# A decoder layer on one Trainium2 core: gated rows and weights of the last six down tiles go into the operand slots of the recursive units

## The chip, the cores and the metric

The kernel runs on one NeuronCore of a Trainium2 chip. The metric is the device time of one execution in microseconds (us), and the median of the runs counts. A time inside an execution is counted from the first instruction of the profiled execution.

## What is computed

One decoder layer runs over 1024 prompt tokens and 8 sample tokens (T = 1032 columns, width 1024). The change is in the last part of it, the gated feed-forward and the second layer norm:

```python
gt, up = jnp.split(h @ w_gate_up, 2, axis=-1)
h = layer_norm(ALPHA * h + (jax.nn.silu(gt) * up) @ w_down, ln2_g, ln2_b)
```

The feed-forward width is 2816, which is 22 tiles of 128 rows. All of it is float32 accuracy.

## The kernel before

**Number format.** TensorE multiplies float32r operands. Each operand x is kept as a pair: `hi`, a rounded copy that ScalarE casts (L79), and `lo = x - hi`, which VectorE subtracts (L80). `split` issues both. A product takes three matmuls: hi by hi, lo by hi and hi by lo (L120 to L122 in `mm3`, L245 to L247 in `fast_product`).

**The recursive units.** Most large products are made by a scheme of seven products on 2 x 2 blocks in place of eight. `gate_up_down` runs 28 such units one after the other: 20 for pairs of gate and up tiles (called `("g", f)`), then four for each of two parts of the down projection, (0, 0) to (0, 3) and (1, 0) to (1, 3). A part covers eight of the 22 gated tiles, and a unit of it makes two of the eight output row tiles. A unit has seven steps i = 0 to 6, each of 2 column halves p by 4 tiles by 3 matmuls of 258 columns. Steps 0, 2, 4 and 6 add into one PSUM bank per half (`ubf`), steps 1 and 5 into a second (`udf`), step 3 has a third (`ucf`). In between the banks are read: `p1s`, `p5s` and `u2s` are ScalarE copies (L271) after steps 0, 1 and 2, L273 on VectorE reads `ucf`, L275 reads `ubf` after step 4, L278 reads `udf` after step 5. So step 4 may not add to `ubf` before `u2s` is taken, and step 6 not before L275 has read it. At its end a unit adds its two row tiles to the running sum `scr_h` in DRAM with two accumulating DMAs on the GpSimd queue (L1425).

**The slots.** The moving operands of the down units lie in eight slots, called homes 0 to 7, each with one pair per column half. Product i of part q lies in home (i - q - 1) mod 8. So in part 1 the homes of steps 0 to 6 are 6, 7, 0, 1, 2, 3 and 4, and home 5, which step 6 of part 0 used, is empty during part 1. Homes 0, 3, 5 and 7 are the tiles of `quarter_pair`, the others are tiles `t1`, `t2`, `t4` and `t6` of the pool `tx`. `down_operand` fills the slots of part 1 during the units (0, 2) and (0, 3), with 14 loads of 516 KB (names `f1...` and `fs`) and 14 splits of 1032 columns.

**The last six tiles.** `LAST = (16, 6)`: gated tiles 16 to 21 are not in the two parts. `down` opens two new pools, `gA` for the six rows (128 x 1032, `gh` and `gl`) and `wl` for the weights, in the space that the slots leave when `tx` and the pools under it are closed. It loads the six rows (L1283), splits them by column chunk (384, 390 and 258 columns, `CH`), and `last_products` then makes for each chunk c and each output row tile m a sum `dl` of 18 matmuls (6 tiles by 3). In chunk 0 it also loads and splits the weights `wl` of tile m (two raw halves of 512 and 256 columns through six raw buffers, L95) and loads the running sum, `acc[m] <- scr_h` (L1309). VectorE adds `dl` to `acc` (L1326), and the layer norm of a chunk runs beside the next chunk. The last chunk has its own norm, `last_layer_norm`, after which the kernel ends.

**What sets the order.** In this part no order is written by hand. A list scheduler orders each engine's instructions by its own estimates, and each engine, and the SP queue that issues the loads, then works strictly in that order: an instruction that waits holds everything behind it on its engine. A new tile waits until the readers of the buffer that it takes over are done. `behind` pins one instruction behind another.

Of the kernel before, what the change touches and what calls it, by code (L numbers as in the profile page):

```python
# [10 lines left out]
F32 = mybir.dt.float32  # L11
# [7 lines left out]
P = 128  # L19
D = 1024  # L20
KT = D // P
# [40 lines left out]
class Builder:  # L62
# [910 lines left out]
    def last_layer_norm(self, n, r, product, gcol, emit):  # L973


        nc, ph = self.nc, self.ph
        ones = self.ones.bitcast(F32)
        tile_ = lambda tag, name, bufs, dt=F32: ph.tile([P, WIDE], dt, tag=tag, name=name, bufs=bufs)[:, :n]
        s1, s2 = tile_("s1", "ls1", 1), tile_("s2", "ls2", 1)
        hi, lo = (ph.tile([P, n], F32R, tag=f"c0{e}", name=f"c0{e}", bufs=1) for e in "hl")  # L980
        e1, e2 = self.bank("t", "le1")[:, :n], self.bank("t", "le2")[:, :n]

        def account(m):
            sq = s2 if m == 0 else tile_("sq", f"lsq{m}", 2)
            nc.scalar.activation(sq, r[m], AF.Square)
            if m == 7:
                return sq
            if m == 1:
                nc.vector.tensor_add(s1, r[0], r[1])
            elif m:  # L990
                nc.vector.tensor_add(s1, s1, r[m])
            if m:
                nc.gpsimd.tensor_add(s2, s2, sq)

        for m in range(KT):
            ps = product(m, last=m < LATE)
            if m in NORM_AT:
                self.norm_step()
            if m >= LATE:
                nc.tensor.matmul(ps, self.shift, hi, start=False, stop=False)  # L1000
                nc.tensor.matmul(ps, self.shift, lo, start=False, stop=True)
            nc.vector.scalar_tensor_tensor(r[m], ps, SHARE, r[m], op0=ALU.mult, op1=ALU.add)
            if m == 1:
                s = tile_("xres", "lc0", 2)
                nc.vector.tensor_add(s, r[0], r[1])
                self.split(hi, lo, s)
            elif m == LATE - 1:
                with self.tc.issue_after(self.last_mm):
                    c0 = self.bank("o", "c0")[:, :n]
                    nc.tensor.matmul(c0, self.shift, hi, start=True, stop=False)  # L1010
                    nc.tensor.matmul(c0, self.shift, lo, start=False, stop=True)
                for k in range(LATE):
                    nc.vector.scalar_tensor_tensor(r[k], c0, SHARE, r[k], op0=ALU.mult, op1=ALU.add)
                    account(k)
            elif m >= LATE:
                sq = account(m)
# [12 lines left out]
        self.norm_step()  # L1029
        for m in range(KT):  # L1030
            nc.vector.tensor_mul(r[m], r[m], rs)
            emit(m, r[m], self.vec[:, gcol + m:gcol + m + 1])
# [190 lines left out]
    def gate_up_down(self, ts):  # L1223
# [23 lines left out]
        for n, (u, i) in enumerate(todo):  # L1247
            if i == 1 and n // 7 + 1 < len(units):
                load(n // 7 + 1)
                with self.tc.issue_after(self.last_load):  # L1250
                    for _ in range(2):
                        next(copies, None)
            if n + ahead < len(todo):
                v, j = todo[n + ahead]
                self.fast_quarter(st[v], j)
            self.fast_step(st[u], i, moving[u[0]], finish[u])
            if i == 6:
                del st[u]
            if i in (1, 4) and sums and next(sums[0], self) is self:
                sums.popleft()  # L1260
            if u[0] == "g" and i == 6 and u[1] in (8, 16):
                sums.append(self.down_sums(u[1] // 8 - 1))
            nxt = 0 if u[0] == "g" else u[0] + 1
            if nxt < FAST:
                if u[1] == last[u[0]][1] - 1 and i == 3:
                    self.down_operand(nxt, 0, moving[nxt])
                if u == last[u[0]] and i < 6:
                    while sums:
                        for _ in sums.popleft():
                            pass  # L1270
                    self.down_operand(nxt, i + 1, moving[nxt])
        for _ in copies:
            pass

    def down(self, ga, wl):

        nc, io = self.nc, self.io
        f0, nf = LAST
        tiles = {j: [ga.tile([P, GS], F32R, tag=f"g{e}{j}", name=f"g{e}{f0 + j}", bufs=1) for e in "hl"]
                 for j in range(nf)}  # L1280
        g = [[tuple(a[:, t0:t0 + n] for a in tiles[j]) for t0, n in CH] for j in range(nf)]
        for j in range(nf):
            nc.sync.dma_start(tiles[j][1][:, :T].bitcast(F32), self.scr["f"][:, f0 + j, :])  # L1283
        last = None
        for c in range(3):
            for j in range(nf):
                hi, lo = g[j][c]
                ins = self.split(hi, lo, lo.bitcast(F32)), self.last_lo
                for a, b in zip(ins, last) if last else ():
                    self.behind(a, b)  # L1290
                last = ins
        acc = [self.zt(f"acc{m}") for m in range(KT)]
        self.last_products(acc, g, wl)

    def last_products(self, acc, g, pool):
        nc, io, ph = self.nc, self.io, self.ph
        self.norm, w = None, []
        f0, nf = LAST
        for c, (t0, n) in enumerate(CH):
            rs = [acc[m][:, t0:t0 + n] for m in range(KT)]  # L1300

            def product(m, last=True, c=c, n=n):
                if c == 0:
                    hi, lo = (pool.tile([P, nf * P], F32R, tag="wl", name=f"wl{e}{m}", bufs=16) for e in "hl")
                    for a, b in ((0, 512), (512, nf * P)):
                        raw = self.half_raw(io["wdn"][m][:, f0 * P + a:f0 * P + b], b - a, f"wl{m}r{a}")
                        self.split(hi[:, a:b], lo[:, a:b], raw[:, :b - a])
                    w.append([(hi[:, k * P:(k + 1) * P], lo[:, k * P:(k + 1) * P]) for k in range(nf)])
                    nc.sync.dma_start(acc[m], self.scr["h"][:, m, :])  # L1309
                ps = self.bank(("mm", "s")[m % 2], f"dl{m}_{c}")[:, :n]  # L1310
                self.mm3(ps, [(w[m][k], g[k][c]) for k in range(nf)], last)
                return ps

            def emit(m, v, scale=1.0, t0=t0, n=n):
# [4 lines left out]
                self.last_layer_norm(n, rs, product, V_G2, emit)  # L1319
                break  # L1320
            s1 = ph.tile([P, WIDE], F32, tag="s1", name=f"o2s{c}", bufs=1)[:, :n]
            for m, r in enumerate(rs):
                ps = product(m)
                if m in NORM_AT:
                    self.norm_step()
                nc.vector.scalar_tensor_tensor(r, ps, SHARE, r, op0=ALU.mult, op1=ALU.add)  # L1326
                if m == 1:
                    nc.vector.tensor_add(s1, rs[0], r)
                elif m > 1:
                    nc.vector.tensor_add(s1, s1, r)  # L1330
            self.norm_start(self.layer_norm(c, rs, s1, V_G2, emit, "n2", c == 1))

    def build(self):
# [15 lines left out]
        with ExitStack() as right:  # L1349
# [25 lines left out]
            self.zbufs = 10  # L1375
            with pool("zf") as self.z:
                with ExitStack() as tx:
                    with pool("lnp") as self.ph:
                        self.lw = QN
                        with pool("tw", "right") as self.tw:  # L1380
                            h = self.out_proj(self.merged)
                        self.tx = tx.enter_context(pool("tx", "right"))
                        ts = self.plain(h)
                    with pool("w1") as self.w1:
                        self.gate_up_down(ts)
                right.close()
                with pool("gA", "right") as ga, pool("wl", "right") as wl, pool("ph5") as self.ph:
                    self.lw = WIDE
                    self.down(ga, wl)


class FinishGate:
# [180 lines left out]
```

## Time and profile before

| what | value |
|---|---|
| runs | 1957.96, 1958.57 and 1963.9 us, median 1958.57 us |
| profiled execution | 1960.02 us, its span 1958.2 us, 1.8 us around the span |
| mean granted TensorE clock | 0.993 |
| TensorE busy | 1908.7 us, 97% of the span |
| VectorE, ScalarE, GpSimd busy | 1389.1, 1001.2 and 110.7 us |
| last unit (1, 3) on TensorE | about 1833.1 to 1853.3 us |
| chunk 0 of the last six tiles | to 1891.98 us, where chunk 1 starts |

The stage that matters is the change-over from the last recursive unit to the plain products of the last six tiles. A busy TensorE is not yet a TensorE at full speed: its matmuls are pipelined, so the distance between the starts of neighbouring matmuls is the measure, and the granted clock stands beside the busy time in the table of stages. The name of a row is output, then inputs, with buffer numbers left out: `dl<-gl,wlh` is a product of the last six tiles, `ubf<-dth,uf_0h` one of a down unit. PEld is TensorE's weight load, and SPq the queue that issues loads and stores.

### The profile page before, as it was taken

What the parts mean: (1) busy time and instruction counts of PE and PEld (TensorE: products, weight loads), DVE (VectorE), ACT (ScalarE), POOL (GpSimd) and SP (SyncE); (2) the same over time, 40 slices, a digit from 0 to 9 for tenths busy, and PEclk for the clock granted to TensorE, in tenths of its full rate; (3) what the DMA queues carried; (4) which work ended last, traced back from release to release, by engine and by line L of the source; (5) the groups of instructions that cost most, each with busy time, mean ns of one, the idle gap of its engine ahead of it and who ended that gap; (6) DMA issues with size and microseconds to landing.
All of it is one profiled execution on the core that took longest, in us unless ns stands there. A gap on an engine that the chain in (4) does not pass through costs nothing.

```text
span 1958.2 us, 38029 instructions
## 1 busy us (share of the span) xinstructions
PE 1908.7 (97%) x14716; PEld 1875.0 (96%) x14716; DVE 1389.1 (71%) x2750; ACT 1001.2 (51%) x2127; POOL 110.7 (6%) x168
## 2 busy tenths in 40 slices
PE   9999999999999999999999999999999999999986
PEld 8999999998999998988999999999999999999986
DVE  7878978887766654388877557776567566956367
ACT  6555565554655544388775234544334343644334
POOL 1000000010000000021220000000000000000101
PEclk9999999999999999999999999999999999999998
DMA  8554545456323376667535351132255345676632
GB/s 314 176 157 161 175 165 192 138 175 204 122 79 130 125 247 204 201 169 210 159 88 160 108 187 52 61 98 88 97 171 186 97 142 184 238 196 169 157 125 87
DMA packets 171638, 303.20 MB, mean 155 GB/s; under 512 B 19569, under 2 KB 86209, under 8 KB 171457
## 3 DMA queue, kind: packets, MB, share of 16 engines
q1 hardware_dynamic: 168384, 290.22, 45.7%
q0 software_dynamic: 3072, 10.55, 2.8%
q8 instruction: 115, 1.88, 0.4%
q14 instruction: 67, 0.54, 0.1%
HBM read 214.79 MB, written 90.09 MB: 156 GB/s over the span
## 4 chain that ended last, share of the span: by engine, by line
PE 83%; DMA 6%; ACT 5%; DVE 4%; issue 1%; SPq 1%; ACTq 0%; DVEq 0%; POOL 0%; POOLq 0%
PE ub L247 5%; PE ub L245 5%; PE ub L246 5%; PE ubfg L245 4%; PE ubfg L246 4%; PE ubfg L247 4%; PE ud L247 2%; PE ud L246 2%; PE ud L245 2%; PE udfg L245 2%; PE udfg L246 2%; PE udfg L247 2%; PE brs L120 2%; PE brs L121 2%; PE brs L122 2%; PE ubf L245 2%
## 5 line engine op out<-in xcount | busy, mean ns | idle before, releaser
L122 PE MATMUL op<-mh,wol 128*128 128x258 f32 x256 | 72.3, 282 | 1.3 <-DVE wol L80 1.3
L120 PE MATMUL op<-mh,woh 128*128 128x258 f32 x256 | 72.5, 283 | 0.0
L121 PE MATMUL op<-ml,woh 128*128 128x258 f32 x256 | 72.1, 282 | 0.0
L599 ACT ACTIVATE bp<-bp,bst 128x257 f32<-128x257 f32 (+1 forms) x128 | 62.8, 493 | 17.3 <-DVE bst L595 17.0
L245 PE MATMUL ub<-th,u_4h 128*128 128x258 f32 x240 | 68.0, 283 | 3.3 <-ACT u2s L271 3.3
L245 PE MATMUL ub<-th,u_0h 128*128 128x258 f32 x240 | 68.2, 284 | 1.7 <-ACT zb L1444 1.7
L245 PE MATMUL ub<-th,u_2h 128*128 128x258 f32 x240 | 68.0, 283 | 0.3 <-ACT p1s L271 0.3
L247 PE MATMUL uc<-th,u_3l 128*128 128x258 f32 x240 | 68.2, 284 | 0.0
L247 PE MATMUL ub<-th,u_2l 128*128 128x258 f32 x240 | 68.2, 284 | 0.0
L247 PE MATMUL ub<-th,u_4l 128*128 128x258 f32 x240 | 68.2, 284 | 0.0
L247 PE MATMUL ub<-th,u_6l 128*128 128x258 f32 x240 | 68.2, 284 | 0.0
L247 PE MATMUL ud<-th,u_1l 128*128 128x258 f32 x240 | 68.2, 284 | 0.0
L247 PE MATMUL ub<-th,u_0l 128*128 128x258 f32 x240 | 68.2, 284 | 0.0
L247 PE MATMUL ud<-th,u_5l 128*128 128x258 f32 x240 | 68.2, 284 | 0.0
L245 PE MATMUL ub<-th,u_6h 128*128 128x258 f32 x240 | 68.0, 284 | 0.0
L245 PE MATMUL ud<-th,u_5h 128*128 128x258 f32 x240 | 67.9, 283 | 0.0
L245 PE MATMUL ud<-th,u_1h 128*128 128x258 f32 x240 | 67.9, 283 | 0.0
L245 PE MATMUL uc<-th,u_3h 128*128 128x258 f32 x240 | 67.8, 282 | 0.0
L246 PE MATMUL ub<-tl,u_0h 128*128 128x258 f32 x240 | 67.7, 282 | 0.0
L246 PE MATMUL ud<-tl,u_1h 128*128 128x258 f32 x240 | 67.6, 282 | 0.0
L246 PE MATMUL ud<-tl,u_5h 128*128 128x258 f32 x240 | 67.6, 282 | 0.0
L246 PE MATMUL ub<-tl,u_6h 128*128 128x258 f32 x240 | 67.6, 282 | 0.0
(876 smaller groups left out, 8224.4 us busy)
## 6 DMA issues: line engine op xcount, KB each, us to landing
ur<-win SPq DMA_DIRECT2D x120, 256.0 KB, 2.9
urfg<-wgu SPq DMA_DIRECT2D x80, 256.0 KB, 2.7
scr_f<-G SPq DMA_DIRECT2D x22, 516.0 KB, 2.8
f<-scr_f SPq DMA_DIRECT2D x16, 516.0 KB, 6.0
fs<-scr_t SPq DMA_DIRECT2D x16, 516.0 KB, 7.1
dck<-cmk SPq DMA_DIRECT2D x32, 256.0 KB, 3.0
dcv<-cmvT SPq DMA_DIRECT2D x32, 256.0 KB, 3.5
st<-scr_q SPq DMA_DIRECT2D x32, 256.0 KB, 4.8
```

Of the source, the lines that this page charges most:

```text
L120: nc.tensor.matmul(ps, sh, mh, start=opens and i == 0, stop=False)
L121: nc.tensor.matmul(ps, sh, ml, start=False, stop=False)
L122: self.last_mm = nc.tensor.matmul(ps, sl, mh, start=False, stop=closes and i == last).ins
L245: mm(sh[:, w], xh, start=opens and k == 0, stop=False)
L246: mm(sh[:, w], xl, start=False, stop=False)
L247: self.last_mm = mm(sl[:, w], xh, start=False, stop=k == 3).ins
L599: nc.scalar.activation(x, x, AF.Exp, bias=st[:, g:g + 1], scale=-1.0, accum_out=st[:, 4 + g:5 + g])
```

## The change

The pools `gA` and `wl` and the method `down` are gone. The rows and the weights of the last six tiles take over the slots of the down units, home by home, while the last units run:

- rows 16 and 17 in home 5 (called in unit (1, 2), step 4), rows 18 and 19 in home 6 and rows 20 and 21 in home 7 (unit (1, 3), steps 0 and 1). A row is loaded whole and split whole, 1032 columns at once, where the split was done by chunk;
- weights of output tiles 0 and 1 in home 0, 2 and 3 in home 1 (unit (1, 3), steps 2 and 4); those of 4 and 5 in home 2 and of 6 and 7 in home 3 from inside the product loop;
- `acc[0]` and `acc[1]` are loaded from the calls after steps 3 and 5, the others from the product loop;
- the pair `hi`, `lo` of the last norm's correction lies in home 4;
- `last_products` runs inside the scope of the slots, and the pool `ph5` opens where the pool `w1` of the units was.

No matmul is added or removed: TensorE has 14471 rows in both programs. ScalarE and VectorE have 12 rows fewer each (18 splits of rows become 6), SP has as many rows as before.

```diff
+            if n >= len(todo) - 10:
+                step = {0: lambda: self.last_rows(5, 0), 3: lambda: self.last_rows(6, 2),
+                        4: lambda: self.last_rows(7, 4), 5: lambda: self.last_weights(0, 0),
+                        6: lambda: self.last_acc(0), 7: lambda: self.last_weights(1, 2),
+                        8: lambda: self.last_acc(1)}.get(n - len(todo) + 10)
+                if step:
+                    step()
...
+    def slot_pairs(self, home, name):
+
+        quarter = {0: 0, 3: 1}.get(home)
+        if quarter is not None:
+            return [self.quarter_pair(p, quarter, name) for p in range(2)]
+        return [tuple(self.tx.tile([P, 4, QN], F32R, tag=f"t{home}", name=f"{name}{e}{p}", bufs=4) for e in "hl")
+                for p in range(2)]
+
+    def last_rows(self, home, j0):
+
+        flat = lambda t: t.rearrange("p k n -> p (k n)")
+        for p, pair in enumerate(self.last_pair(home)):
+            hi, lo = map(flat, pair)
+            self.nc.sync.dma_start(lo.bitcast(F32), self.scr["f"][:, LAST[0] + j0 + p, :])
+            self.split(hi, lo, lo.bitcast(F32))
+            self.g.append([tuple(a[:, t0:t0 + n] for a in (hi, lo)) for t0, n in CH])
...
-                right.close()
-                with pool("gA", "right") as ga, pool("wl", "right") as wl, pool("ph5") as self.ph:
-                    self.lw = WIDE
-                    self.down(ga, wl)
+                    with pool("ph5") as self.ph:
+                        self.lw = WIDE
+                        self.last_products()
```

**Place one, the last unit on ScalarE and VectorE.** In ScalarE's order before, from the second half of step 1 of unit (1, 3) on, where `p5s`, `u2s` and `zbf` are the reads of that unit's banks and `uf13_6h` is its last weight:

```order
L271 ACTIVATE p5sf13_0_23660<-udf13_0_23647 128x258
L79 CAST uf13_6h_23711<-urf13_11_23405 128x512
L271 ACTIVATE p5sf13_1_23675<-udf13_1_23662 128x258
L271 ACTIVATE u2sf13_0_23695<-ubf13_0_23611 128x258
L271 ACTIVATE u2sf13_1_23709<-ubf13_1_23626 128x258
L1421 ACTIVATE zbf13_23744<-ubf13_0_23611 128x258
L1421 ACTIVATE zbf13_23744<-ubf13_1_23626 128x258
L79 CAST wlh0_23900<-wl0r0_23902 128x512
```

ScalarE's order of the change at the same place, where `g6` and `g7` are the rows in homes 6 and 7 and `wl0h0` is the first weight in home 0:

```order
L271 ACTIVATE p5sf13_0_23680<-udf13_0_23667 128x258
L79 CAST g6h0_23651<-g6l0_23652 128x1032
L79 CAST uf13_6h_23761<-urf13_11_23405 128x512
L271 ACTIVATE p5sf13_1_23695<-udf13_1_23682 128x258
L79 CAST wl0h00_23741<-wl0r0_23745 128x512
L79 CAST g7h20_23697<-g7l20_23698 128x1032
L271 ACTIVATE u2sf13_0_23725<-ubf13_0_23621 128x258
L271 ACTIVATE u2sf13_1_23739<-ubf13_1_23636 128x258
```

Two casts of loaded rows now stand ahead of `u2sf13_0`, and the second halves of those rows follow behind. VectorE's order of the change over the same steps, where before no row of a split stood between `uf13_6l` and L273:

```order
L80 TENSOR_TENSOR g6l0_23652<-g6l0_23652,g6h0_23651 128x1032
L80 TENSOR_TENSOR wl0l00_23742<-wl0r0_23745,wl0h00_23741 128x512
L80 TENSOR_TENSOR uf13_6l_23762<-urf13_11_23405,uf13_6h_23761 128x512
L80 TENSOR_TENSOR g7l20_23698<-g7l20_23698,g7h20_23697 128x1032
L80 TENSOR_TENSOR wl0l00_23742<-wl0r512_23749,wl0h00_23741 128x256
L80 TENSOR_TENSOR g6l1_23654<-g6l1_23654,g6h1_23653 128x1032
L80 TENSOR_TENSOR wl0l10_23744<-wl1r0_23753,wl0h10_23743 128x512
L80 TENSOR_TENSOR g7l30_23700<-g7l30_23700,g7h30_23699 128x1032
L80 TENSOR_TENSOR wl0l10_23744<-wl1r512_23757,wl0h10_23743 128x256
L273 SCALAR_TENSOR_TENSOR zaf13_23765<-ucf13_0_23766,p1sf13_0_23634 128x258
L273 SCALAR_TENSOR_TENSOR zaf13_23765<-ucf13_1_23780,p1sf13_1_23649 128x258
L275 SCALAR_TENSOR_TENSOR zbf13_23796<-ubf13_0_23621,p5sf13_0_23680 128x258
```

Eight splits moved ahead of the unit's last reads. **Place two, the start of the last products on TensorE.** Before, three output tiles are worked on at once, row by row as the rows come in:

```order
L120 MATMUL dl0_0_23911<-gh16_23837,wlh0_23900 128x384
L120 MATMUL dl1_0_23942<-gh16_23837,wlh1_23931 128x384
L121 MATMUL dl0_0_23911<-gl16_23838,wlh0_23900 128x384
L122 MATMUL dl0_0_23911<-gh16_23837,wll0_23901 128x384
L121 MATMUL dl1_0_23942<-gl16_23838,wlh1_23931 128x384
L120 MATMUL dl2_0_23974<-gh16_23837,wlh2_23963 128x384
```

In the change one tile is finished before the next begins, the row in home 5 first and those in home 7 last:

```order
L120 MATMUL dl0_0_23904<-g5h21_23541,wl0h00_23741 128x384
L121 MATMUL dl0_0_23904<-g5l21_23542,wl0h00_23741 128x384
L122 MATMUL dl0_0_23904<-g5h21_23541,wl0l00_23742 128x384
L120 MATMUL dl0_0_23904<-g5h31_23543,wl0h00_23741 128x384
L121 MATMUL dl0_0_23904<-g5l31_23544,wl0h00_23741 128x384
L122 MATMUL dl0_0_23904<-g5h31_23543,wl0l00_23742 128x384
```

Tile `dl0` now needs all six rows from its first 18 matmuls on. **Place three, the SP queue.** Before, the six rows follow one another behind the first three `acc` loads:

```order
L1309 DMA acc2_23893<-scr_h_82 128x1032
L1283 DMA gl16_23838<-scr_f_83 128x1032
L1283 DMA gl17_23840<-scr_f_83 128x1032
L1283 DMA gl18_23842<-scr_f_83 128x1032
L1283 DMA gl19_23844<-scr_f_83 128x1032
L1283 DMA gl20_23846<-scr_f_83 128x1032
L1283 DMA gl21_23848<-scr_f_83 128x1032
L95 DMA wl3r0_23997<-wdn 128x512
```

In the change the rows of home 5 stand 15 rows further up, behind the loads of unit (1, 1), and the other four stand among the weights and ahead of every `acc`:

```order
L95 DMA wl2r0_23827<-wdn 128x512
L1302 DMA g6l0_23652<-scr_f_83 128x1032
L1302 DMA g7l20_23698<-scr_f_83 128x1032
L1302 DMA g6l1_23654<-scr_f_83 128x1032
L1302 DMA g7l30_23700<-scr_f_83 128x1032
L95 DMA wl2r512_23831<-wdn 128x256
L95 DMA wl3r0_23835<-wdn 128x512
L95 DMA wl3r512_23839<-wdn 128x256
L95 DMA wl4r0_23995<-wdn 128x512
L1321 DMA acc0_23794<-scr_h_82 128x1032
L1321 DMA acc1_23869<-scr_h_82 128x1032
```

The loads of the last four rows and of the last weights now come before the sums that they are added to.

More of the change, by code (lines that the diff above doesn't have):

```diff
@@ L979, in last_layer_norm @@
         s1, s2 = tile_("s1", "ls1", 1), tile_("s2", "ls2", 1)
-        hi, lo = (ph.tile([P, n], F32R, tag=f"c0{e}", name=f"c0{e}", bufs=1) for e in "hl")
+        hi, lo = (t.rearrange("p k n -> p (k n)")[:, :n] for t in self.slot_pairs(4, "c0")[0])
         e1, e2 = self.bank("t", "le1")[:, :n], self.bank("t", "le2")[:, :n]
@@ L1272, in gate_up_down @@
         for _ in copies:
             pass
-    def down(self, ga, wl):
-        nc, io = self.nc, self.io
-        f0, nf = LAST
[L1279 to L1293, printed above, removed]
@@ L1295, in last_products, with last_pair @@
-    def last_products(self, acc, g, pool):
+    def last_pair(self, home):
+        if home in (5, 7):
+            kh = int(home == 5)
+            return [self.quarter_pair(2 + p, kh, f"g{home}") for p in range(2)]
+        return self.slot_pairs(home, f"g{home}")
+    def slot_pairs(self, home, name):
[4 more added lines that the diff above has]
+                for p in range(2)]
@@ new lines, in last_rows, with last_weights @@
+    def last_rows(self, home, j0):
[5 more added lines that the diff above has]
+            self.g.append([tuple(a[:, t0:t0 + n] for a in (hi, lo)) for t0, n in CH])
+    def last_weights(self, home, m0):
+        flat = lambda t: t.rearrange("p k n -> p (k n)")
+        f0, nf = LAST
+        for p, pair in enumerate(self.slot_pairs(home, f"wl{home}")):
+            m = m0 + p
+            hi, lo = map(flat, pair)
+            for a, b in ((0, 512), (512, nf * P)):
+                raw = self.half_raw(self.io["wdn"][m][:, f0 * P + a:f0 * P + b], b - a, f"wl{m}r{a}")
+                self.split(hi[:, a:b], lo[:, a:b], raw[:, :b - a])
+            self.wl.append([(hi[:, k * P:(k + 1) * P], lo[:, k * P:(k + 1) * P]) for k in range(nf)])
@@ L1296, in last_products, with last_acc, product @@
+    def last_acc(self, m):
+        self.acc.append(self.zt(f"acc{m}"))
+        self.nc.sync.dma_start(self.acc[m], self.scr["h"][:, m, :])
+    def last_products(self):
         nc, io, ph = self.nc, self.io, self.ph
-        self.norm, w = None, []
+        self.norm, w, g, acc = None, self.wl, self.g, self.acc
         f0, nf = LAST
         for c, (t0, n) in enumerate(CH):
[L1300 to L1309, printed above, removed]
+            rs = []
+            def product(m, last=True, c=c, t0=t0, n=n, rs=rs):
+                if c == 0 and m >= len(w):
+                    self.last_weights(m // 2, m)
+                if c == 0 and m >= len(acc):
+                    self.last_acc(m)
@@ L1310, in product @@
                 ps = self.bank(("mm", "s")[m % 2], f"dl{m}_{c}")[:, :n]
                 self.mm3(ps, [(w[m][k], g[k][c]) for k in range(nf)], last)
+                rs.append(acc[m][:, t0:t0 + n])
                 return ps
@@ L1321, in last_products @@
             s1 = ph.tile([P, WIDE], F32, tag="s1", name=f"o2s{c}", bufs=1)[:, :n]
-            for m, r in enumerate(rs):
+            for m in range(KT):
                 ps = product(m)
+                r = rs[m]
                 if m in NORM_AT:
@@ L1377, in build @@
                 with ExitStack() as tx:
+                    self.g, self.wl, self.acc = [], [], []
                     with pool("lnp") as self.ph:
```

## The prediction

> **What bounds the kernel now.** I read the chain of work that ended last first, then the busy times by stage, then the starts of single matmuls, and last who waited for whom. The page's chain and its table of engines:
>
> ```profile
> PE 1908.7 (97%) x14716; PEld 1875.0 (96%) x14716; DVE 1389.1 (71%) x2750; ACT 1001.2 (51%) x2127; POOL 110.7 (6%) x168
> ...
> PE 83%; DMA 6%; ACT 5%; DVE 4%; issue 1%; SPq 1%; ACTq 0%; DVEq 0%; POOL 0%; POOLq 0%
> ```
>
> TensorE carries the chain, so only time in which it stands or runs slowly can be won. The table of stages (stretch, its length, busy time of PE, PEld, DVE, ACT, POOL, then the granted clock, the DMA share and GB/s) shows where that is:
>
> ```profile
> 1740.00:1780.00 40.00, 40.00 (x336) 40.00 (x335) 33.55 (x47) 26.41 (x45) 3.47 (x4) 1.00 0.95 284
> 1833.10:1853.30 20.20, 20.20 (x170) 20.15 (x168) 5.33 (x10) 4.66 (x11) 1.74 (x2) 1.00 0.71 184
> 1853.30:1892.00 38.70, 31.69 (x147) 29.61 (x146) 22.22 (x47) 14.42 (x35) 0.87 (x1) 0.87 0.65 210
> 1892.00:1932.00 40.00, 39.97 (x258) 39.53 (x257) 34.44 (x68) 17.54 (x32) 0.00 (x0) 1.00 0.11 41
> ```
>
> The first row is a stretch in the middle of the down units, the second the last unit, the third chunk 0 of the last six tiles, the fourth the work behind it. Only the third has a hole: 7.0 us idle, and a clock of 0.87. Its size follows from starts of matmuls, in TensorE's timeline (start, duration, operation):
>
> ```profile
> 1834.44 0.28 PE L247 MATMUL ubf<-dth,uf_0l 128*128 128x258 f32 x1
> 1837.32 0.28 PE L247 MATMUL udf<-d11h,uf_1l 128*128 128x258 f32 x1
> 1844.63 0.28 PE L245 MATMUL ubf<-dth,uf_4h 128*128 128x258 f32 x1
> 1850.42 0.28 PE L245 MATMUL ubf<-dth,uf_6h 128*128 128x258 f32 x1
> 1853.17 0.28 PE L247 MATMUL ubf<-dth,uf_6l 128*128 128x258 f32 x1
> 1855.15 1.21 PE L120 MATMUL dl<-gh,wlh 128*128 128x384 f32 x2 [1.70 <-ACT gh L79]
> 1862.08 0.62 PE L120 MATMUL dl<-gh,wlh 128*128 128x384 f32 x2 [0.77 <-ACT gh L79]
> 1877.09 0.53 PE L121 MATMUL dl<-gl,wlh 128*128 128x384 f32 x1
> 1877.41 0.53 PE L122 MATMUL dl<-gh,wll 128*128 128x384 f32 x1
> 1883.11 0.34 PE L120 MATMUL dl<-gh,wlh 128*128 128x384 f32 x1
> 1891.98 0.34 PE L120 MATMUL dl<-gh,wlh 128*128 128x390 f32 x1
> ```
>
> From 1883.11 to 1891.98 nothing is waited for: 51 matmuls in 8.87 us, 0.174 us apart. Chunk 0 has 8 tiles of 18, which is 144 matmuls or 25.05 us. From step 4 (1844.63) to step 6 (1850.42) are two steps, 5.79 us: 24 matmuls in 2.89 us, 0.12 us apart, so chunk 0 could begin at 1853.17 + 0.12 = 1853.29 and end at 1878.34. It ends at 1891.98: **13.64 us** are lost. The waits of TensorE, and of ScalarE behind them, from the end of the unit on (total, times, longest):
>
> ```profile
> PE dl L120 <- ACT gh L79: 4.4, 3, 1.9
> PE dl L122 <- DVE wll L80: 1.8, 1, 1.8
> PE dl L120 <- ACT wlh L79: 0.8, 2, 0.6
> ...
> ACT gh L79 <- DMA gl<-scr_f: 8.0, 4, 3.3
> ACT wlh L79 <- DMA wl6r<-wdn: 3.9, 1, 3.9
> ACT wlh L79 <- DMA wl7r<-wdn: 2.9, 1, 2.9
> ```
>
> The three waits of TensorE make the 7.0 us. The other 6.64 us are the slow clock: at 1877.09 and 1877.41 the starts are 0.32 us apart in place of 0.174. ScalarE in turn waits for loads. The SP queue and the chain show which:
>
> ```profile
> 1849.06 4.64 SPq L1283 DMA_DIRECT2D gl<-scr_f  x6
> ...
> 1852.28 14.35 DMA gl<-scr_f
> ```
>
> The six rows are issued from 1849.06 on, since they take the space of slots that are read until then; the last lands at 1866.63, 13.3 us into a chunk that needs it at once.
>
> **The change part by part.** *Removed:* the late rows, and the late weights 6 and 7 behind them. If neither is waited for, 13.64 us go: 7.0 of waits and 6.64 of clock.
>
> *Rows in home 5.* Two loads, two casts and two subtractions go into the units before. Their sizes are those of `fs`, the whole rows that were loaded and split there before (duration min/median/max in ns; then landing times of the loads in us, for `fs` and for `gl`):
>
> ```profile
> L79 ACT CAST dth<-fs x4: 1054/1056/1062, 1766.5 to 1774.7; 128x1032 fp32r<-128x1032 f32 x4
> L80 DVE TENSOR_TENSOR dtl<-fs,dth x4: 1229/1232/1234, 1767.6 to 1776.6; 128x1032 fp32r<-128x1032 f32 x4
> DMA to landing us min/median/max: 5.4/7.0/8.6
> ...
> DMA to landing us min/median/max: 3.7/6.8/14.3
> ```
>
> So 2.1 us on ScalarE and 2.5 us on VectorE, which had 13.6 and 6.4 us free of 40 in the first stage row, with TensorE busy 40.00 of 40.00 and 284 GB/s moved. I take nothing. If that cover is gone, one pair stands ahead of a unit's bank read and holds TensorE by at most 1.06 + 1.23 = 2.3 us.
>
> *Rows in homes 6 and 7.* The first half of home 6 is free after its last reader, 1834.44 + 0.28 = 1834.72, that of home 7 after 1837.32 + 0.28 = 1837.60. Loads are issued there, ahead of every `acc`, and do not wait for the end of the unit. What is new is a wait: ScalarE takes `u2sf13_0` only behind the casts of `g6l0` and `g7l20`, and TensorE's step 4, due at 1844.63, needs it. VectorE reaches L275 of the first half only behind eight splits, and step 6, due at 1850.42, needs that. Before, nothing stood ahead of either. Further prices, a read of a bank on each engine and the two pieces of a weight on each (mean ns in the second part of a row):
>
> ```profile
> 1840.51 0.39 ACT L271 ACTIVATE u2sf<-ubf 128x258 f32<-128x258 f32 x1 [0.59 <-PE ubf L247]
> 1846.28 0.43 DVE L275 SCALAR_TENSOR_TENSOR zbf<-ubf,p5sf 128x258 f32<-128x258 f32 x1 [1.02 <-PE ubf L247]
> L80 DVE TENSOR_TENSOR wll<-wl0r,wlh 128x512 fp32r<-128x512 f32 x1 | 0.7, 693 | 3.3 <-ACT wlh L79 3.3
> L80 DVE TENSOR_TENSOR wll<-wl0r,wlh 128x256 fp32r<-128x256 f32 x1 | 0.4, 418 | 0.0
> L79 ACT CAST wlh<-wl0r 128x512 fp32r<-128x512 f32 x1 | 0.6, 610 | 0.0
> L79 ACT CAST wlh<-wl0r 128x256 fp32r<-128x256 f32 x1 | 0.4, 406 | 0.0
> ```
>
> Let L be the time to landing of `g7l20`. Its cast ends at 1837.60 + L + 1.06 and `u2sf13_0` 0.39 us later, at 1839.05 + L: step 4 is late by L - 5.58. On VectorE from that cast on stand three rows of 1.23 us, a weight piece of 0.69, two of 0.42, and three bank reads of 0.43, 6.51 us in all: 1845.17 + L, so step 6 is late by L - 5.25. The delays are not added: the second includes the first. L lies between 3.7 and 14.3 us; I take **6.8**, the median of the loads of this very tensor (`fs`: 7.0). The stall is 1.55 us, 1.22 at step 4 and 0.33 at step 6; at 8.6, the worst `fs`, 3.35. The engines have room in all: VectorE 5.33 + 4 x 1.23 + four weight pieces for two tiles 4.4 = 14.7 of 20.2 us, ScalarE 4.66 + 4.24 + 4.1 = 13.0.
>
> *Weights.* Tiles 0 to 3 come with the unit. Tile m is due at 1853.29 + 3.13 m, so 6 at 1872.1 and 7 at 1875.2. Homes 2 and 3, which 4 to 7 use, are free at about 1847.5 and 1850.42, the ends of steps 4 and 5. If weights 6 are issued by 1853.3 and land as late as the latest row, 14.3 us, they are split at 1867.6 + 2.1 = 1869.7. I take nothing; the dear end is the second rival.
>
> *Sums.* `acc` now comes behind the rows. The last two wait for the unit's accumulating DMAs, as before. Those took (KB each, us to landing), and `acc` loads took (min/median/max):
>
> ```profile
> scr_h<-zaf POOLq DMA_DIRECT2D x1, 516.0 KB, 10.3
> scr_h<-zbf POOLq DMA_DIRECT2D x1, 516.0 KB, 11.4
> ...
> DMA to landing us min/median/max: 3.8/4.6/12.9
> ```
>
> From 1853.5: 11.4 + 4.6 makes 1869.5, and with 12.9 1877.8, still ahead of the last tile's end at 1878.34 + 1.55. Nothing.
>
> *Behind chunk 0* TensorE is busy 39.97 of 40.00 us, and the instructions there are the same, so what chunk 0 gains is kept whole. The twelve splits fewer lie beside that work.
>
> **Sum:** 13.64 - 1.55 = 12.1 us. The profiled execution took 1960.02 us (span 1958.2 and 1.8 around it), so 1947.9 of its kind. It is 1.45 us above the median of 1958.57: **1946.5 us**.
>
> [...]
>
> **The rivals.**
>
> *The clock falls in the stall.* In chunk 0 the granted clock went down after some idles and not after others:
>
> ```profile
> 1855.15:1858.00 2.85, 2.78 (x8) 2.51 (x9) 2.85 (x7) 2.34 (x6) 0.00 (x0) 0.59 1.03 298
> 1862.00:1866.00 4.00, 1.98 (x10) 1.53 (x10) 0.64 (x2) 0.54 (x2) 0.00 (x0) 0.99 1.03 328
> ```
>
> Behind the idle of 1.70 us (at 1855.15) it was 0.59, behind the one of 0.77 us (at 1862.08) 0.99. A stall of 1.22 us lies between, a little nearer the harmless one. With three such stretches in 6.64 us one costs 2.2, and the result is 1948.7.
> [...]
>
> *The DMA engines become the bound.* The last unit and chunk 0 moved 20.2 x 184 + 38.7 x 210 = 11.8 MB; two rows (128 x 1032 x 4 bytes, 0.53 MB each) leave this stretch, 10.8 MB stay. To be in by about 1876 from 1834.7 on they need 262 GB/s. For it: at 210 GB/s, the rate of the third stage row, they take 51.4 us, to 1886.1, which saves 5.9 us: 1952.7. Against it: 284 GB/s held for 40 us in the first stage row and 328 in the row above, and the third row has a DMA share of 0.65.
>
> *Late rows.* With L at 14.3 the stall is 9.05 us and one slow stretch 2.2: 2.4 us saved, 1956.2. For it, that landing was seen; against it, six rows were in flight behind three `acc` then, and four among small weights now.
>
> *Slower.* The wait for one row, ahead of `u2sf13_0` and of the splits before L275, holds both engines and so TensorE in the unit, where nothing stood before. It decides from L - 5.25 = 13.64, that is L = 18.9 us; with 2.2 for the clock from 16.7. At L = 22 the kernel takes 1958.57 + 16.75 + 2.2 - 13.64 = 1963.9. The largest landing in these rows is 14.3.
>
> That the change does nothing is ruled out by the order: rows and weights stand ahead of the unit's last reads.
>
> **How the numbers follow.** Forecast 0.55, clock 0.20, DMA 0.13, late rows 0.08, slower 0.04. With L from 5.25 down the stall is nothing and the time 1945.0; 1944 leaves a margin of what the fastest run lay under the median (0.6). Above, 3.35 with a slow stretch is 1950.5, the DMA case 1952.7: the range is 1944 to 1953. A measurement of this kernel tells about 0.3% from no change, 5.9 us: faster is below 1952.7. Half of the DMA case and half of the late rows fall inside: faster 0.86, same 0.10, slower 0.04.
>
> **What would show it.** Right: the first `dl` matmul 0.1 to 0.2 us behind the last `ubf`, its clock at 1.00, 25 us to the first 390-column matmul, and one wait for `u2s` or for L275 of 1 to 2 us in the last unit. Wrong: TensorE waiting for `wlh` or `wll` of tiles 4 to 7 (DMA), a wait of over 4 us at step 4 (late rows), a slow clock in the unit, or TensorE waiting in units (1, 0) to (1, 2), where home 5 is filled.

## The result, and the profile after

The changed kernel takes 1945.91 us in the median of six runs (1942.13 to 1952.14), the kernel before 1958.09 us (six runs, 1955.59 to 1963.9). The ratio is 0.9938 with a 95% interval from 0.9917 to 0.9958: 0.6% faster, 12.2 us between the medians. The forecast was 1946.5 us. The profiled execution took 1946.82 us, its span is 1945.0 us.

The table of stages of the changed kernel, cut at its own points: the last unit, chunk 0, and 40 us behind it. Columns as before: the stretch, its length, busy time of PE, PEld, DVE, ACT and POOL, granted clock, DMA share, GB/s.

```profile
1834.39:1855.01 20.62, 20.53 (x170) 20.32 (x169) 13.36 (x22) 12.27 (x24) 0.86 (x1) 1.00 0.86 264
1855.01:1880.15 25.14, 25.14 (x146) 25.14 (x145) 10.74 (x22) 3.58 (x8) 1.79 (x2) 1.00 0.69 213
1880.15:1920.15 40.00, 39.99 (x258) 39.56 (x257) 34.37 (x68) 17.53 (x32) 0.00 (x0) 1.00 0.12 41
```

The hole is gone: chunk 0 is TensorE work from end to end, at a clock of 1.00 in place of 0.87, and takes 25.14 us in place of 36.83. VectorE and ScalarE are busy for 13.36 and 12.27 us in the last unit, where they had 5.33 and 4.66. TensorE's timeline shows the seams:

```profile
1845.79 0.28 PE L247 MATMUL ucf<-dth,uf_3l 128*128 128x258 f32 x1
1846.16 0.39 PE L245 MATMUL ubf<-dth,uf_4h 128*128 128x258 f32 x1
1852.08 0.34 PE L245 MATMUL ubf<-dth,uf_6h 128*128 128x258 f32 x1
1854.89 0.28 PE L247 MATMUL ubf<-dth,uf_6l 128*128 128x258 f32 x1
1855.01 0.34 PE L120 MATMUL dl<-g5h,wl0h 128*128 128x384 f32 x1
1880.15 0.34 PE L120 MATMUL dl<-g5h,wl0h 128*128 128x390 f32 x1
```

The first product of the last tiles starts 0.12 us behind the unit's last matmul, the pitch of the unit itself. Step 4 starts 0.37 us behind its neighbour in place of 0.12: 0.25 us of stall. From step 4 to step 6 go 5.92 us in place of 5.79. The whole unit, from its first matmul to its last, takes 20.50 us in place of 20.07: the queue in the unit costs 0.43 us here.

One measure serves for all runs below: **the stretch from the first matmul of the last unit to the first one of chunk 1.** It was 58.88 us before (1833.10 to 1891.98) and is 45.76 us (1834.39 to 1880.15), so 13.12 us are won. Single times of one kernel scatter by 3 to 12 us, and the stages ahead take part in that (over the profiles of this study the last unit starts anywhere from 1828.97 to 1834.39 us); the two stretches of each kernel lie within 0.4 us (table below).

The span shrank by 13.2 us. That is 13.12 in the stretch, less 1.29 because the last unit starts that much later, plus 1.37 behind chunk 0, where the sums of the last norm ran at half pace before and at full pace in this profile. First the row of before, then that of the change:

```profile
1941.23 1.23 PE L1017 MATMUL le<-ls,ones 128*128 128x258 f32 x2 [3.14 <-DVE ls L991]
```

```profile
1929.43 0.70 PE L1017 MATMUL le<-ls,ones 128*128 128x258 f32 x2 [3.12 <-DVE ls L991]
```

The idle ahead of them is the same, 3.14 and 3.12 us. Whether this belongs to the change is one of the questions below.

### The profile page after: what moved, and what is told of

Its sections match the earlier page's. It is cut to its first block, busy times and chain, and to the rows that moved or that the text cites. A ratio compares the mean times of both kernels' runs of the same rounds, so it can differ in the third digit from the quotient of the medians.

```text
span 1945.0 us, 38003 instructions
## 1 busy us (share of the span) xinstructions
PE 1901.7 (98%) x14716; PEld 1870.0 (96%) x14716; DVE 1387.5 (71%) x2738; ACT 999.9 (51%) x2115; POOL 113.7 (6%) x168
## 4 chain that ended last, share of the span: by engine, by line
PE 82%; DMA 6%; DVE 5%; ACT 4%; issue 1%; SPq 0%; ACTq 0%; DVEq 0%; POOL 0%; POOLq 0%
PE ub L247 5%; PE ub L245 5%; PE ub L246 5%; PE ubfg L245 4%; PE ubfg L246 4%; PE ubfg L247 4%; PE ud L247 2%; PE ud L246 2%; PE ud L245 2%; PE udfg L245 2%; PE udfg L246 2%; PE udfg L247 2%; PE brs L120 2%; PE brs L121 2%; PE ubf L245 2%; PE brs L122 2%
## 5 line engine op out<-in xcount | busy, mean ns | idle before, releaser
L246 PE MATMUL ub<-tl,u_4h 128*128 128x258 f32 x240 | 67.6, 282 | 0.0
```

The costliest lines, as they stand in the source:

```text
L246: mm(sh[:, w], xl, start=False, stop=False)
```

## The experiments

| kernel | rows | weights of tiles 0 to 3 | stretch, us | median, us |
|---|---|---|---|---|
| before, two profiles | late | late | 58.88, 59.25 | 1958.09 |
| change, two profiles | early | early | 45.76, 46.07 | 1945.91, 1944.30 |
| e3 splits later | early | early | 45.33 | 1946.93 |
| e4 row twice | early, one delayed | early | 47.19 | 1948.13 |
| e1 rows late | behind two `acc` | early | 48.31 | 1951.55 |
| e2 weights late | early | late | 50.64 | 1947.91 |
| e5 rows later | behind three `acc` | early | 52.77 | 1953.96 |
| e6 both late | behind three `acc` | late | 53.35 | 1951.09 |
| e9 late homes | in late slots | early | 52.87 | 1955.72 |
| e10 late homes and weights | in late slots | late | 52.81 | 1954.94 |
| e11 filled, e3 with a filler in the last norm | early | early | 45.34 | 1949.04 |
| e12 before, splits of chunks 1 and 2 later | late | late | 53.88 | 1952.47 |

The kernel before, run beside them, had a median between 1958.09 and 1960.58 us.

**Both kernels once more (e7, e8).** No edit.

> The changed kernel once more. The first profile had the sums of the last norm (le) at full clock and the profile before had them at half: 15.57 against 16.97 us from the first le to the end. If that is chance, this profile may show either, and 45.8 us from the start of the last unit to the end of chunk 0 again; if the change causes it, 15.6 us again. Time 1943 to 1949 us.

> The kernel before once more, for its trace: 58.9 us from the start of the last unit to the end of chunk 0 if the loss is the program's and not one run's; the same waits for gl and wl. The start of the last unit may move by 1 to 4 us either way, and the last sums may run at full clock: 15.6 or 17.0 us to the end.

The stretches came again: 46.07 and 59.25 us. (The median of e7 is 1944.30 us; e8 is a single execution of 1956.79 us.) What fills the lost time did not. Chunk 0 of the second profile of before:

```profile
1851.10:1890.16 39.06, 29.13 (x146) 26.14 (x145) 22.35 (x47) 14.53 (x35) 0.87 (x1) 0.96 0.65 208
```

and TensorE's waits in it:

```profile
PE dl L120 <- ACT gh L79: 5.5, 3, 1.9
PE dl L120 <- ACT wlh L79: 2.3, 2, 2.1
PE dl L122 <- DVE wll L80: 1.8, 1, 1.8
```

It waits for 9.6 us where the first profile waited for 7.0, with a mean clock of 0.96 where that had 0.87, and ends within 0.4 us of the same length. So in these two profiles the slow clock was no second loss beside the waits: the one with the slower clock waited less, and the end came at the same place. That the loads and splits set the end is what the next runs try.

The sums of the last norm ran at full pace in this profile of before too, from the first `le` to the end 15.63 us (16.97 in the first), and the change had 15.57 and 15.68. Sums at half pace, with 1.23 us in the first row, also show in the profiles of e1, e2 and e3, which have the change's slots. The 1.37 us behind chunk 0 are chance and not the change's.

**Rows late alone (e1, e5).** The calls stand behind the loop, and each load is queued behind that of `acc1`, in e5 behind that of `acc2`.

```diff
-step = {0: lambda: self.last_rows(5, 0), 3: lambda: self.last_rows(6, 2),
-        4: lambda: self.last_rows(7, 4), 5: ...
+step = {5: ...
...
+for home, j0 in ((5, 0), (6, 2), (7, 4)):
+    self.last_rows(home, j0)
...
+    self.behind(load, self.acc_load)
```

> The changed kernel, but the six row loads are queued behind the load of acc1, so that they start at about 1851 us as they did before; the weights of the first tiles still come early. Theory A (the rows' lateness is the loss): the last row lands 10 to 14 us after its issue, TensorE waits in the first tiles for g rows, chunk 0 takes 36 to 39 us in place of 25.1, and the time is 11 to 14 us above the change, 1957 to 1960 us. Rival (early weights bring half or more of the gain): 1949 to 1953 us, with waits below 5 us in chunk 0.

> As e1_rows_late, but the rows are queued behind the third acc load, the place they had before; weights early. In e1 the stretch from the start of the last unit to the end of chunk 0 was 48.3 us against 45.8 in the change and 58.9 before. Theory B (late rows alone do not make the loss, since TensorE goes over to the rows and the three or four tiles that are there): 50 to 53 us, a time 4 to 7 us above the change. Theory A (the rows' lateness is the loss): 57 us or more, 11 to 13 us above the change.

In the stretch e1 loses 2.55 us against the change and not 11 to 14. TensorE's waits in it:

```profile
PE dl L120 <- ACT g6h L79: 1.8, 1, 1.8
PE dl L121 <- DVE g5l L80: 0.6, 1, 0.6
```

The scheduler lets TensorE work on several tiles with the rows that are there. But its rows were issued from 1845.93 us on, 8 us before the end of the unit, earlier than meant. e5 loses 7.0 us; its rows too came early, from 1845.66 us with the unit ending at 1853.4. A better measure of lateness is when the last row is cast. Counted from the unit's first matmul, that cast began at 33.55 us before, at 29.08 in e1 and at 32.31 in e5. So the theory that the rows' lateness by itself makes the loss fails by e5 already, whose last row is 1.2 us earlier than before while the stretch is 6.1 us shorter; e9 has them as late as before. An early issue moved the cast less than itself: counted in the same way, the first row is issued at 15.96 us before and at 12.42 in e5.

**Weights late alone, and both (e2, e6).** Every weight split of the last tiles is queued behind the unit's last read of a bank (`zbf`), and the calls for weights inside the units are gone. e6 has the rows' edit of e5 as well.

```diff
-5: lambda: self.last_weights(0, 0), 7: lambda: self.last_weights(1, 2),
...
-self.split(hi[:, a:b], lo[:, a:b], raw[:, :b - a])
+self.behind(self.split(hi[:, a:b], lo[:, a:b], raw[:, :b - a]), self.last_late)
...
-self.b.nc.scalar.mul(dst, ps, -SHARE)
+self.b.last_late = self.b.nc.scalar.mul(dst, ps, -SHARE).ins
```

> The changed kernel with its early rows, but every weight split of the last six tiles is queued on ScalarE behind the last unit's last bank read (zbf), where it stood before. Theory A: only the first tile waits, for the first weight: zbf ends near 1855.6, cast and subtraction take 1.3 us, so the first dl matmul starts about 2 us later than in the change, and one slow stretch of 1.5 to 2.2 us may follow: 1948 to 1950 us. Rival (early weights bring half or more of the gain): 1952 us or more.

> The rows as in e5 and the weight splits as in e2, in the change's buffers: rows and weights are both as late as before. Theory B (the two together make the loss: late rows push the loads of weights 3 to 7 behind them, and the products wait first for rows, then for weights): 57 to 60 us from the start of the last unit to the end of chunk 0, 1957 to 1961 us, as before the change. Rival (something else in the change, the whole splits or the one-tile order, brings a part): 50 to 55 us, 1950 to 1955 us.

e2 loses 4.9 us in the stretch, more than the 2 to 4 expected. TensorE waited twice, and ScalarE for one load:

```profile
PE dl L120 <- ACT wl1h L79: 1.5, 1, 1.5
PE dl L120 <- ACT wl0h L79: 1.0, 1, 1.0
```

```profile
ACT wl1h L79 <- DMA wl3r<-wdn: 9.0, 1, 9.0
```

In SP's queue `wl3r` now stands behind seven `acc` loads, which are issued from 1843.69 to 1857.90 us; its own issue is at 1858.00. e6 gives 53.35 us: 7.6 of the 13.1 us come back, and no more. But its rows did not come late: they were issued from 1843.42 us on with the unit ending at 1852.15, and the last one was cast 28.12 us behind the unit's first matmul, earlier than in e1. Of TensorE's waits in it 0.2 us are for rows and 3.8 for weights. So e6 is no trial of both at once; e10 below is one. A part of nearly 6 us was unnamed.

**Rows in slots that come free late (e9, e10).** Slots exchanged: rows in homes 2, 3 and 4, weights in 5, 6, 7 and 0; the pair of the last norm's correction moves to home 1.

```diff
-step = {0: lambda: self.last_rows(5, 0), 3: lambda: self.last_rows(6, 2), ...
+step = {3: lambda: self.last_weights(5, 0), 4: lambda: self.last_weights(6, 2),
+        6: lambda: self.last_acc(0), 7: lambda: self.last_rows(2, 0),
+        8: lambda: (self.last_acc(1), self.last_rows(3, 2)),
+        9: lambda: self.last_rows(4, 4)}.get(n - len(todo) + 10)
```

e10 has the weights' edit of e2 as well.

> The changed kernel with the slots exchanged: the six rows go into homes 2, 3 and 4, which are free only after steps 4, 5 and 6 of the last unit, and the weights into homes 5, 6, 7 and 0 (so the weights are early, and their names are g5 to g7). The rows then start between 6 us before and the end of the unit, as late as before the change. Theory B: 53 to 56 us from the start of the last unit to the end of chunk 0 (52.8 in e5, 58.9 before), 1953 to 1956 us. Theory A (late rows alone make the whole loss): 57 us or more, 1957 us or more.

> As e9, with every weight split behind the last unit's last bank read, and so the loads of weights 3 to 7 behind the rows as before. Theory B (late rows, and weight loads behind them, are the whole loss, and the order by tile and the whole splits bring nothing): 57.5 to 60.5 us for the same stretch, 1957 to 1960 us, the time before the change. Rival (the rest of the change has a part of its own): 56 us or less, 1955 us or less.

52.87 and 52.81 us. In e9 the last row is now issued at 1849.54 us, 0.4 us behind the unit's end, and cast 34.95 us behind the unit's first matmul; in e10 the cast is at 33.31 us (33.55 before). TensorE waits in e9 for rows,

```profile
PE dl L120 <- ACT g4h L79: 3.0, 1, 3.0
PE dl L120 <- ACT g2h L79: 1.7, 1, 1.7
PE dl L121 <- DVE g2l L80: 0.3, 1, 0.3
```

5.0 us in all; behind the wait of 3.0 us the granted clock was 0.87 from 1865.02 to 1867.00 us and 0.50 from there to 1869.00. The stretch is 7.1 us longer than in the change. Early weights bring nothing while the rows are late: e9 and e10 differ by 0.06 us. e10 goes against the theory that late rows and late weights together are the whole loss: 6 us are still missing to before.

**The missing part (e12).** What is in before and in none of these? Its rows are split by chunk, and `behind` chains the 18 splits into one sequence. ScalarE's timeline of before:

```profile
1866.65 4.88 ACT L79 CAST gh<-gl 128x384 fp32r<-128x384 f32 x13 [0.77 <-DMA gl<-scr_f]
1871.44 0.92 ACT L79 CAST wlh<-wl3r 128x512 fp32r<-128x512 f32 x2
...
1877.89 0.92 ACT L79 CAST wlh<-wl6r 128x512 fp32r<-128x512 f32 x2 [3.87 <-DMA wl6r<-wdn]
```

As soon as the last row has landed, 13 casts follow: one for chunk 0 and the twelve of chunks 1 and 2, which nobody needs for 20 us yet. The cast of `wl3` stands behind them, and so does its subtraction on VectorE:

```profile
1874.41 0.69 DVE L80 TENSOR_TENSOR wll<-wl3r,wlh 128x512 fp32r<-128x512 f32 x1
```

It ends at 1875.10 us. There are six raw buffers, so `wl6r` takes over that of `wl3r`, and SP issues it right then:

```profile
1875.13 1.14 SPq L95 DMA_DIRECT2D wl6r<-wdn  x2
```

e12 is the kernel before with these twelve splits queued behind the last weight:

```diff
-for c in range(3):
+def rows(c):
     for j in range(nf):
         ...
+rows(0)
...
+if m == KT - 1:
+    self.last = weight
+    self.rows(1)
+    self.rows(2)
```

> The kernel before, with one change of order: the twelve splits of the rows for chunks 1 and 2, which stood on ScalarE and VectorE between the rows of chunk 0 and the weights of tiles 3 to 7 (13 casts in one stretch of 4.88 us from 1866.65 on, the cast of wl3 after it at 1871.44), now stand behind the last weight. Rows and weights are loaded as before. Theory C (those splits hold the weights, their raw buffers, and so the loads of weights 6 and 7, and this is the part of the loss that e10 didn't bring back): 52 to 55 us from the start of the last unit to the end of chunk 0 (58.9 before, 52.8 in e10), 1952.5 to 1955 us. Rival (the part is the space that all six rows wait for at once): 58 us or more, 1957 us or more.

53.88 us, 5.0 us less than before; the median is 1952.47 us against 1959.47 beside it, ratio 0.9966 [0.9952, 0.9979]. `wl6r` is issued at 1866.00 us. ScalarE's timeline shows the weights directly behind the rows of chunk 0:

```profile
1863.95 0.51 ACT L79 CAST gh<-gl 128x384 fp32r<-128x384 f32 x1 [0.76 <-DMA gl<-scr_f]
1864.63 0.93 ACT L79 CAST wlh<-wl3r 128x512 fp32r<-128x512 f32 x2 [0.16 <-DMA wl3r<-wdn]
...
1871.56 0.62 ACT L79 CAST wlh<-wl6r 128x512 fp32r<-128x512 f32 x1 [1.33 <-DMA wl6r<-wdn]
...
1876.49 4.47 ACT L79 CAST gh<-gl 128x390 fp32r<-128x390 f32 x12
```

and TensorE's waits for `wlh` and `wll` are gone; only those for the rows are left:

```profile
PE dl L120 <- ACT gh L79: 4.1, 3, 1.9
```

Its last row is cast 33.40 us behind the unit's first matmul, as late as before, and behind chunk 0 the later splits cost nothing that can be seen: 65.07 us to the end, 64.84 in the second profile of before. So the third cause is shown by itself. What separates e12 (53.88) from e10 (52.81), 1.1 us, was not tried; among others, the splits of whole rows and the order of the products on TensorE differ between them.

**The price of a wait in the unit (e3, e4).** e3 calls `last_rows` behind the loop without a pin. The loads are queued where the change has them, since the scheduler issues a load when its slot is free, wherever the call stands; but the splits now come behind the bank reads. e4 loads the first row of home 7 twice, one after the other, and pins `u2sf` behind that row's cast:

```diff
+if home == 7 and p == 0:
+    self.nc.sync.dma_start(lo.bitcast(F32), self.scr["f"][:, 0, :])
 self.nc.sync.dma_start(lo.bitcast(F32), self.scr["f"][:, LAST[0] + j0 + p, :])
...
+    if i == 2 and p == 0 and getattr(self, "row_cast", None):
+        self.behind(ins, self.row_cast)
```

> The changed kernel with last_rows called behind the unit in the program: the loads are queued at the same places, but ScalarE and VectorE now take the bank reads u2s and L275 ahead of most row splits. Theory A: the wait at step 4 (0.25 us in the change) is gone, step 6 starts on time, and the first tile still finds its rows: 1944 to 1947 us, no difference that the times can show. Rival (early splits are needed): TensorE waits 1 us or more for g7 in the first tile.

> The changed kernel with the first load of home 7 made twice, one after the other (first another row, then the right one), and u2s of the last unit pinned behind the cast of that row as in the change: the time to landing of the row about doubles, from 6 to 11 or 12 us. Theory A (u2s is late by L - 5.58): step 4 waits 5.5 to 7 us in the last unit, a slow stretch of 1.5 to 2.2 us follows, 1953 to 1955 us. Rival (the wait for a row inside the unit is hidden): 1946 us.

e3: 45.33 us, the unit in 20.07 as before the change, chunk 0 in 25.14. The stall of 0.43 us is gone, which the times (1946.93 us) can't show. e4: 47.19 us. The second load took only 3.8 us, so that the row landed 9.7 us after its first issue, and not after 11 or 12. From the chain of work that ended last (start, length):

```profile
1836.55 5.88 DMA g7l<-scr_f
...
1842.49 3.78 DMA g7l<-scr_f
```

and TensorE's timeline behind step 3:

```profile
1843.54 0.28 PE L247 MATMUL ucf<-dth,uf_3l 128*128 128x258 f32 x1
1843.66 0.28 PE L245 MATMUL udf<-d15h,uf_5h 128*128 128x258 f32 x1
...
1845.82 0.28 PE L245 MATMUL udf<-d15h,uf_5h 128*128 128x258 f32 x1
1847.69 0.39 PE L245 MATMUL ubf<-dth,uf_4h 128*128 128x258 f32 x1 [1.59 <-ACT u2sf L271]
```

Step 4 starts 15.55 us behind the unit's first matmul in place of 11.53 before, so it is 4.0 us late. But the order on TensorE is another one in e4: 19 matmuls of step 5, which do not need `u2sf`, stand ahead of step 4 and fill 2.3 us of that. The unit takes 21.93 us in place of 20.07, and chunk 0 again 25.14. So a row that comes later makes step 4 later by as much; but of the 4.0 us only 1.86 are paid, since the scheduler had put other work in front, and nothing is paid behind the unit.

**A filled gap in the last norm (e11).** e3 with 24 matmuls on a constant ahead of `le`.

```diff
+with self.tc.issue_after(self.last_mm):
+    fill = self.bank("mm", "fill")
+    for _ in range(FILL):
+        nc.tensor.matmul(fill[:, :P], self.ones, self.ones, start=True, stop=True)
 nc.tensor.matmul(e1, ones, s1, start=True, stop=False)
```

> e3 with 24 matmuls of 128 columns on a constant between the last product and the sums of the last norm (le), where TensorE otherwise stands for 3.1 us; their result is not used. If the sums sometimes run at half clock because TensorE stood, they now always run at 0.6 us a pair, 15.6 us to the end in place of 15.6 to 17.0: 1943 to 1946 us, about 0.7 us below e3 in the mean, which the times hardly show but the trace does. If the clock does not depend on it, half-clock sums show again.

The sums ran at 0.60 us a pair, as expected, but so they did without a filler, behind an idle of 3.1 us, in both profiles of the change and in the second of before; one profile does not show that the filler did it. And from the first `le` to the end it is 16.76 us, not 15.6. The order on ScalarE is another one too: seven rows of the chunk before now stand ahead of the read of `le`, which starts at 1932.80 us, with the last `le` matmul started at 1929.95. The median, 1949.04 us, is no better than e3's.

## Why the prediction was right, point by point

**What bounds the kernel: right in size, incomplete in cause.** The loss of 13.64 us, from the pitch of undisturbed matmuls, was almost exactly what chunk 0 gave back: 25.14 us measured, 25.05 forecast. The step that failed is the account of it, that "the six rows are issued from 1849.06 on" and that the late weights lay "behind them". With the rows late 7.1 us are lost (e9, e10 against the change), whether the weights are early as in e9 or late as in e10; with early rows, late weights alone cost 4.9 us (e2). About 5 more hang on twelve splits of chunks 1 and 2 that stood between the rows and the weights (e12); the prediction counted them as "twelve splits fewer" that "lie beside that work", at no price. 1.1 us are not assigned. And the issue alone did not make the rows late: the DMA share of before is 1.03 from 1855.15 to 1858.00 us, 1.04 from there to 1862.00, 1.03 to 1866.00 and 1.04 to 1868.00, while the rows were landing, so what part a late issue has and what part DMA engines as busy as that was not separated. It read ScalarE's wait for `wl6r` as a late load and didn't ask why that load was issued at 1875 us, when rows had been landing until 1866.6. The sum came out because the change removes every one of these causes, named or not; that was luck as far as the cause goes. The medians agree to 0.6 us with the forecast, which is closer than runs that spread over 10 us can bear: the sum had 12.1 us, the stretch gave 13.1.

**Waits and clock as two terms: wrong as an account.** 7.0 and 6.64 us were added. The 6.64 were never all clock: a mean clock of 0.87 over 38.70 us is a loss of 5.0 us at most, and 1.6 us stay without a name. The second profile of before lost 14.0 us, 9.6 of them in waits, and its mean clock of 0.96 over 39.06 us is 1.6 us at most. In these two profiles the sum stays within 0.4 us while its parts move.

**Rows in home 5 at nothing: right.** Units (1, 0) to (1, 2) have no wait of TensorE; the trace lists none from 1700 to 1882 us in the change's first profile, and in the second only one of 0.4 us, for `u2sf` in unit (1, 3).

**The stall in the unit: right mechanism, too dear.** 1.55 us were forecast with a landing of 6.8 us. The rows are

```profile
1838.80 0.33 SPq L1302 DMA_DIRECT2D g7l<-scr_f  x1
```

```profile
1844.76 1.06 ACT L79 CAST g7h<-g7l 128x1032 fp32r<-128x1032 f32 x1 [1.16 <-DMA g7l<-scr_f]
1845.72 0.66 ACT L271 ACTIVATE u2sf<-ubf 128x258 f32<-128x258 f32 x2
```

so L is 5.96 us at most, and by the forecast's own rule step 4 is late by 0.38 us; measured 0.25. The unit takes 20.50 us in place of 20.07, and 20.81 in the second profile: 0.43 and 0.74 us, where the sign named for the forecast was a wait of 1 to 2 us. The term that was too large is L, 6.8 for 5.96 us. e4 bears the rule out far from there: with L = 9.7 step 4 should be 4.1 us late and was 4.0. But that all of this lateness becomes a stall holds only while TensorE's order has nothing to put in front, as e4 had. The room of VectorE was reckoned as 14.7 us in the unit and that of ScalarE as 13.0, measured 13.36 and 12.27; the 4.4 us there called "four weight pieces for two tiles" are the price of eight pieces, of four tiles.

**Weights and sums at nothing: right.** `wl6r` was issued at 1856.18 and cast at 1869.25; the first product of tile 6 runs at 1873.88.

**The rivals.** The DMA engines had room: 264 GB/s in the unit and 213 in chunk 0, with shares of 0.86 and 0.69, and TensorE waited for no weight. Late rows and the slower case did not come. No slow stretch followed the stall of 0.25 us, which is too short to judge that rival; e4 is the better trial, 1.6 us of wait and a clock of 1.00 behind it. That is one profile; the last section has a wait of the same size with a slow stretch.

## What to carry to other kernels

When one engine waits for a load, ask when the load was issued and what held it: for `wl6r` it was not the traffic but a raw buffer, held by a split that stood behind twelve others that nobody needed yet. Before operands are moved to come earlier, put the splits in the order of need; e12 wins 5.0 of the 13.1 us by that alone. And where a list scheduler sets the order, the place of a load's call decided little here: in e3 the buffer that a load takes over decided when it was issued, in e1 and e5 the pins did. The splits did move with the call, though, and that took the stall of 0.43 us away.

## What the runs showed of the hardware that was not expected

The clock after an idle is not set by its length alone. Behind the same idle of 1.70 us at the start of chunk 0 the granted clock was 0.59 in the first profile of before, from 1855.15 to 1858.00 us; in the second,

```profile
1852.96:1855.00 2.04, 1.96 (x8) 1.31 (x8) 2.04 (x5) 1.66 (x4) 0.00 (x1) 1.00 0.98 281
```

it was 1.00, and 1.00 again from 1855.00 to 1857.00 us. In the first profile TensorE started again at 1855.15 us. From 1855.00 to 1855.50 us the granted clock was still 1.00, in the next half microsecond 0.65, in each of the six half microseconds from 1856.00 to 1859.00 us 0.50, then 0.94, and 1.00 from 1859.50 to 1864.00. Behind a wait of 1.6 us in e4 the clock stayed at 1.00 too, from 1847.69 to 1854.10 us, and behind one of 3.6 us in e5, which ended at 1866.66 us, it fell:

```profile
1868.00:1870.00 2.00, 2.00 (x7) 2.00 (x8) 1.03 (x2) 0.48 (x2) 0.00 (x0) 0.54 1.03 399
```

So the idle of 1.70 us was followed by a slow stretch in one of two cases. What else decides it was not shown.
